# A hybrid layer on one core: the recurrence is solved in blocks, a convolution group moves to the front, and its taps and sums move to VectorE

## The chip, the cores and the metric

The kernel runs on 1 core of a Trainium2 chip. A core has four compute engines that work side by side and wait for one another through semaphores: TensorE (PE, matrix products), VectorE (DVE), ScalarE (ACT) and GpSimd (POOL). Transfers are issued from queues, here mostly that of SyncE (SP). Every engine takes its instructions in the order in which they were written into its queue, so an instruction that waits holds up all that stand behind it on that engine. The metric is the time of one execution in microseconds (us), as the device measures it; lower is better.

## The reference, cut to what matters

The input is 512 frames of 2048 channels. The first half of the layer is the part that the change touches:

```
h = rms_norm(x);  [u | v | g] = h @ W_in                # 1024 channels each
A:  bu = B u;  h[t] = lam * h[t-1] + bu[t]               # complex, 64 groups x 64 states, per frame
    y  = gelu(Re(C h) + D u);  y = y * sigmoid(y @ W_glu)
B:  z  = v * sigmoid(g);  z = causal depthwise conv of 31 taps;  layer norm over 1024 channels;  silu
x = x + rms_norm(concat(A, B) @ W_out)
```

A feed-forward part with its own up and down projections and a convolution of 3 taps follows; it is not changed.

## The kernel before, in words

Channels lie on the 128 partitions and frames along the free dimension, so a tile of 128x512 holds 128 channels of all frames. Every large product runs in three passes (`gemm`, L121 to L123): a weight block `wraw` of 128x1024 is split by ScalarE into a rounded part `wh` (L101) and by VectorE into the rest `wl` (L102), and TensorE adds `wh` times both parts of the activations and `wl` times the first. One such block, a *weight tile* below, feeds 24 products of 512 columns. There are two buffers each of `wh` and `wl` and three of `wraw`. Up to the start of the second part of the output projection VectorE splits 72 weight tiles: 48 of `w_in` (six groups of four 128-channel outputs, 8 tiles each), 8 of `w_glu`, 16 of the first half of `w_out`.

The input projection has two groups for `u` (state space) and four for `v` and `g` (value and gate). In the program the `u` groups come first (`pu0`, L222, then L467), then the four value and gate groups (L575). The norm factor `rx` (L281) is ready once the first group's input is through.

The state space works in chunks of T = 8 frames, NC = 64 of them. GpSimd computes the powers of lambda and the coefficient tables `cst`, `cy`, `cf` (helpers at L245 and L249). The products of B are spread over partitions by small transfers (`wscr`, L404) and multiplied out on VectorE (L413 to L418, 48 instructions, tiles `bx`, `by`, `btw`). `u_evac` (L447) scales a group by `rx`, sends it through memory into another layout and fills the state tile `st`, [128, 2, 32, 64] (real and imaginary, 32 pairs, 64 chunks). Then the recurrence walks over the chunks:

```python
    for c in range(NC - 1):                                    # 63 steps, L472
        ve.tensor_tensor(out=sa, in0=st[:, :, :, c], in1=lr8, op=MUL)
        ve.tensor_tensor(out=sx, in0=st[:, ::-1, :, c], in1=lam8[:, 1:3], op=MUL)
        ve.tensor_tensor(out=sa, in0=sa, in1=st[:, :, :, c + 1], op=ADD)
        scan_end = ve.tensor_tensor(out=st[:, :, :, c + 1], in0=sa, in1=sx, op=ADD).ins
```

Behind it the states go to memory (`sscr`, L516) and come back in another layout (L521); eight blocks of products (L530, L531) and a GELU give the output of the state space, which goes through memory again (`yscr`, L539) into `yall` (L541). L585 splits it into `yh` and `yl` for the `w_glu` product.

`vg_evac` (L546) evacuates a value and gate group (L551, L554 on VectorE, sigmoid on ScalarE), multiplies both on GpSimd (L557) and runs 31 taps for each of its two 128-channel blocks. The first tap is on ScalarE, the others are one VectorE instruction each (L572) that is not issued before `scan_end`. Of the eight blocks, block 3 (`PCONV`) takes another way: ScalarE scales (`pt`, L568) and GpSimd adds (L569). The layer norm sums over the blocks on GpSimd (L608, L610, L623); L617, L628 and L632 on VectorE finish it.

What sets the order: the program is written as above with priorities (weight splits, evacuations and the coefficient chain are preferred), and a scheduler fixes each engine's order before the run.

Of the kernel before, what the change touches and what calls it, by code (L numbers as in the profile page):

```python
# [32 lines left out]
PCONV = (3,)  # L33
# [26 lines left out]
def layer_kernel(ctx, tc, a, out):  # L60
# [110 lines left out]
    lam8 = const.tile([P, 3, NQ], F32, name="lam8")  # L171
# [16 lines left out]
    for i in range(2):  # L188
        for o, v in ((xts[0][:, i], a["x"][:, i]), (w0[:, S * i:S * i + S], a["w_in"][0, 0][:, S * i:S * i + S])):
# [32 lines left out]
    pu0 = gemm(wing[0], xrhs, w0, xuse)  # L222
# [322 lines left out]

    def vg_evac(ps, i0):  # L546
        zs = []
        for i in range(2):
            with tc.high_priority(offset=EPRI):
                gt = evt()  # L550
                ve.tensor_tensor(out=gt, in0=ps[2 * i + 1], in1=rx, op=MUL)  # L551
                se.activation(out=gt, in_=gt, func=AF.Sigmoid)
                vt = evt()
                ve.tensor_tensor(out=vt, in0=ps[2 * i], in1=rx, op=MUL)  # L554
            z = cv.tile([P, CK - 1 + S], F32, name="z", bufs=5)
            ge.memset(z[:, 0:CK - 1], 0.0)
# [1 line left out]
            zs.append(z)
        for k in range(CK):
            for i in range(2):  # L560
                c = i0 + i
                w = convw[:, c, k:k + 1]
                zk = zs[i][:, k:k + S]
                if k == 0:
                    se.activation(out=csb[:, c, :], in_=zk, func=AF.Copy, scale=w)
# [464 lines left out]
```

## Time and profile before

| | us |
|---|---|
| median of three runs (2088.94 to 2093.76) | 2091.67 |
| profiled execution, its own time | 2092.54 |
| span in that execution, first to last instruction | 2090.6 |
| TensorE busy | 1956.1 (94%) |
| VectorE busy | 1506.4 (72%) |
| ScalarE busy | 827.8 (40%) |
| GpSimd busy | 343.8 (16%) |
| mean granted clock of TensorE | 0.970 |

The profile is of one execution. Busy time is counted per engine, and a share over the whole span mixes parts with different limits: the changed part lies in the first 556 us, and the windows of these are what to read. The granted clock is a share of full speed: 1.00 is 2.4 GHz, and a stretch at the lower of the two levels, 1.2 GHz, counts as 0.50. The profiled time and the span differ by 1.9 us.

### The profile page before, as it was taken

How to read it: one execution, taken by the hardware profiler on the slowest of the kernel's cores; microseconds unless marked ns; L12 is line 12 of the kernel's file. 1: busy time of each engine (PE TensorE's matmuls, PEld its weight loads, DVE VectorE, ACT ScalarE, POOL GpSimd, SP SyncE). 2: the span in 40 equal slices, each digit the busy share in tenths (PEclk: the TensorE clock that was granted, in tenths of full speed). 3: DMA queues.
4: the chain of work that ended last, by engine and by line, in shares of the span. 5: the costliest groups of instructions: out<-in, count | busy, mean ns of one | idle time of the engine just before them, and what ended most of it. 6: DMA issues, size and time to landing. Idle time of an engine off the chain costs nothing. (4 is left out here: it accounts for less than half of the span.)

```text
span 2090.6 us, 30295 instructions
## 1 busy us (share of the span) xinstructions
PE 1956.1 (94%) x12070; PEld 1746.7 (84%) x12070; DVE 1506.4 (72%) x1947; ACT 827.8 (40%) x1050; POOL 343.8 (16%) x367
## 2 busy tenths in 40 slices
PE   7867988799998889999999999999999999999995
PEld 6656777678786779999999999999997888888884
DVE  5388999999536898787777878778783555555545
ACT  5111233433545544444444444444444322222223
POOL 6655143401122000000000000000000000000004
PEclk9988999999998999999999999999999999999997
DMA  6674667422226547767677676776736333333322
GB/s 211 172 222 156 213 186 209 122 86 96 91 93 175 160 152 222 204 190 210 182 199 195 194 210 184 201 197 191 207 117 225 123 131 113 119 119 123 101 94 88
DMA packets 141357, 338.80 MB, mean 162 GB/s; under 512 B 31392, under 2 KB 52896, under 8 KB 140704
## 3 DMA queue, kind: packets, MB, share of 16 engines
q1 hardware_dynamic: 123072, 289.41, 41.6%
q0 software_dynamic: 13392, 45.36, 12.5%
q10 hardware_dynamic: 4752, 2.11, 0.5%
q8 instruction: 94, 1.54, 0.3%
q14 instruction: 47, 0.39, 0.1%
HBM read 304.12 MB, written 32.70 MB: 161 GB/s over the span
## 5 line engine op out<-in xcount | busy, mean ns | idle before, releaser
L102 DVE TENSOR_TENSOR wl<-wraw,wh 128x1024 fp32r<-128x1024 f32 (+1 forms) x193 | 251.0, 1301 | 243.1 <-ACT wh L101 237.8
L101 ACT CAST wh<-wraw 128x1024 fp32r<-128x1024 f32 (+1 forms) x193 | 201.7, 1046 | 509.0 <-PE mm L122 455.1
L123 PE MATMUL mm<-hl,wl 128*128 128x512 f32 x832 | 312.0, 408 | 60.8 <-DVE wl L102 60.7
L815 PE MATMUL mm<-hl,wl 128*128 128x256 f32 x1280 | 362.9, 284 | 4.4 <-DVE wl L808 4.4
L813 PE MATMUL mm<-hl,wh 128*128 128x256 f32 x1280 | 363.1, 284 | 2.1 <-ACT wh L807 1.5
L814 PE MATMUL mm<-hl,wh 128*128 128x256 f32 x1280 | 362.9, 283 | 0.0
L121 PE MATMUL mm<-hl,wh 128*128 128x512 f32 x832 | 333.7, 406 | 24.9 <-ACT wh L101 16.1
L122 PE MATMUL mm<-hl,wh 128*128 128x512 f32 x832 | 331.8, 402 | 0.0
L121 PE MATMUL mm<-hidh,wh 128*128 128x512 f32 x704 | 275.1, 392 | 4.6 <-ACT hidh L912 4.6
L122 PE MATMUL mm<-hidl,wh 128*128 128x512 f32 x704 | 274.8, 390 | 0.0
L123 PE MATMUL mm<-hidh,wl 128*128 128x512 f32 x704 | 258.4, 390 | 0.0
L123 PEld LDWEIGHTS mm<-hl,wl 128*128 128x128 f32 x832 | 162.6, 196 | 105.6 <-DVE wl L102 70.6
L815 PEld LDWEIGHTS mm<-hl,wl 128*128 128x128 f32 x1280 | 246.4, 193 | 4.6 <-DVE wl L808 4.6
L813 PEld LDWEIGHTS mm<-hl,wh 128*128 128x128 f32 x1280 | 246.4, 193 | 2.6 <-ACT wh L807 1.7
L814 PEld LDWEIGHTS mm<-hl,wh 128*128 128x128 f32 x1280 | 246.4, 193 | 0.0
L121 PEld LDWEIGHTS mm<-hl,wh 128*128 128x128 f32 x832 | 162.4, 196 | 61.4 <-ACT wh L101 18.2
L808 DVE TENSOR_TENSOR wl<-s,wh 128x1024 fp32r<-128x1024 f32 x117 | 143.2, 1224 | 87.5 <-ACT wh L807 87.5
L807 ACT CAST wh<-wraw 128x1024 fp32r<-128x1024 f32 x120 | 125.8, 1048 | 183.5 <-PE mm L814 180.7
L807 ACT CAST wh<-s 128x1024 fp32r<-128x1024 f32 x117 | 122.8, 1049 | 175.9 <-DVE s L864 92.7
L122 PEld LDWEIGHTS mm<-hl,wh 128*128 128x128 f32 x832 | 162.2, 195 | 35.7 <-issue 0.6
L572 DVE SCALAR_TENSOR_TENSOR csb<-z,c_conv_w,csb 128x512 f32<-128x512 f32 x210 | 182.3, 927 | 0.0
L808 DVE TENSOR_TENSOR wl<-wraw,wh 128x1024 fp32r<-128x1024 f32 x120 | 146.7, 1223 | 24.8 <-ACT wh L807 21.9
(277 smaller groups left out, 3541.1 us busy)
## 6 DMA issues: line engine op xcount, KB each, us to landing
wraw<-in_ffn_w_down SPq DMA_DIRECT2D x88, 512.0 KB, 3.2
wraw<-in_ffn_w_quad SPq DMA_DIRECT2D x80, 512.0 KB, 6.2
s<-in_ffn_w_quad SPq DMA_DIRECT2D x78, 512.0 KB, 3.3
s<-in_ffn_w_quad POOLq DMA_DIRECT2D x78, 512.0 KB, 7.9
wraw<-in_w_in SPq DMA_DIRECT2D x47, 512.0 KB, 4.7
rb<-in_ffn_w_quad SPq DMA_DIRECT2D x40, 512.0 KB, 7.6
wraw<-in_w_out SPq DMA_DIRECT2D x32, 512.0 KB, 3.3
fscr<-tmp SPq DMA_DIRECT2D x44, 256.0 KB, 5.2
```

Source lines behind the costliest of these rows:

```text
L101: se.copy(out=h[:, o], in_=raw[:, o])
L102: ve.tensor_tensor(out=l[:, o], in0=raw[:, o], in1=h[:, o].bitcast(F32), op=SUB)
L121: pe.matmul(ps[m], wh[:, kk, m, :], xh, start=k == 0, stop=False)
L122: pe.matmul(ps[m], wh[:, kk, m, :], xl, start=False, stop=False)
L123: pe.matmul(ps[m], wl[:, kk, m, :], xh, start=False, stop=k == nk - 1)
L572: ve.scalar_tensor_tensor(out=csb[:, c, :], in0=zk, scalar=w, in1=csb[:, c, :], op0=MUL, op1=ADD)
L807: se.copy(out=h, in_=raw)
L808: ve.tensor_tensor(out=l, in0=raw, in1=h.bitcast(F32), op=SUB)
L813: pe.matmul(o, h[:, k, :], xh_[:, k, :], start=first and k == 0, stop=False, skip_group_check=True)
L814: pe.matmul(o, h[:, k, :], xl_[:, k, :], start=False, stop=False, skip_group_check=True)
L815: pe.matmul(o, l[:, k, :], xh_[:, k, :], start=False, stop=last and k == 7, skip_group_check=True)
```

## The change

Four things change together.

1. **Blocked recurrence.** A table `lp` holds the first eight powers of lambda to the 8th (18 more small products on GpSimd and one sign change). The recurrence runs over eight blocks of eight chunks: first inside all blocks at once (7 steps of 4 instructions, each on 512 elements per partition in place of 64), then from block to block (7 steps of 4, again 512). 252 instructions become 56.
2. **Order.** The first value and gate group is the first group of the input projection; both `u` groups follow. Its gate (`vg_gate`) comes right behind `rx`, and its taps write a tile of their own (`csb0`) and no longer have to wait for the end of the recurrence (`c > 1` alone does).
3. **Taps and gates on VectorE.** The 30 taps of block 3 that ScalarE and GpSimd shared and the eight products of value and gate move to VectorE.
4. **Norm sums on VectorE.** The seven sums over blocks and the seven over squares move there from GpSimd.

```diff
-    pu0 = gemm(wing[0], xrhs, w0, xuse)
+    pv0 = gemm(wing[2], xrhs, w0, xuse)
...
     rx = rsqrt_bcast([ssq], D)
+    def vg_gate(ps):
+        zs = []
+        for i in range(2):
+            with tc.high_priority(offset=EPRI):
+                gt = evt()
+                ve.tensor_tensor(out=gt, in0=ps[2 * i + 1], in1=rx, op=MUL)
+                se.activation(out=gt, in_=gt, func=AF.Sigmoid)
+                vt = evt()
+                ve.tensor_tensor(out=vt, in0=ps[2 * i], in1=rx, op=MUL)
+            z = zp.tile([P, CK - 1 + S], F32, name="z", bufs=4)
+            ge.memset(z[:, 0:CK - 1], 0.0)
+            ve.tensor_tensor(out=z[:, CK - 1:], in0=vt, in1=gt, op=MUL)
+            zs.append(z)
+        return zs
+    def cs_(c):
+        return csb0[:, c, :] if c < 2 else csb[:, c - 2, :]
+    def vg_taps(zs, i0):
+        for k in range(CK):
+            for i in range(2):
+                c = i0 + i
+                w = convw[:, c, k:k + 1]
+                zk = zs[i][:, k:k + S]
+                if k == 0:
+                    se.activation(out=cs_(c), in_=zk, func=AF.Copy, scale=w)
+                else:
+                    with ExitStack() as order:
+                        if c > 1:
+                            order.enter_context(tc.issue_after(scan_end))
+                        ve.scalar_tensor_tensor(out=cs_(c), in0=zk, scalar=w, in1=cs_(c), op0=MUL, op1=ADD)
+    zs0 = vg_gate(pv0)
...
+    for n in (1, 2, 4):
+        o, x = slice(n, 2 * n), slice(0, n)
+        yr, yi = (lp[:, c, :, n - 1:n].broadcast_to([P, NQ, n]) for c in (0, 2))
+        tt(pa[:, :, 0:n], lp[:, 0, :, x], yr, MUL)
...
-    u_evac(pu0, 0)
+    u_evac(gemm(wing[0], xrhs), 0)
     u_evac(gemm(wing[1], xrhs), 4)
...
-    for c in range(NC - 1):
...
+    sb = st.rearrange("p r q (s i) -> p r q s i", i=NB8)
+    for i in range(1, NB8):
+        sa = sc.tile([P, 2, NQ, NS8], F32, name="sa")
+        sx = sc.tile([P, 2, NQ, NS8], F32, name="sx")
+        ve.tensor_tensor(out=sa, in0=sb[:, :, :, :, i - 1],
+                         in1=lp[:, 0:1, :, 0:1].broadcast_to([P, 2, NQ, NS8]), op=MUL)
+        ve.tensor_tensor(out=sx, in0=sb[:, ::-1, :, :, i - 1],
+                         in1=lp[:, 1:3, :, 0:1].broadcast_to([P, 2, NQ, NS8]), op=MUL)
+        ve.tensor_tensor(out=sa, in0=sa, in1=sb[:, :, :, :, i], op=ADD)
+        ve.tensor_tensor(out=sb[:, :, :, :, i], in0=sa, in1=sx, op=ADD)
+    for b in range(1, NS8):
+        sa = sc.tile([P, 2, NQ, NB8], F32, name="sa")
+        sx = sc.tile([P, 2, NQ, NB8], F32, name="sx")
+        ve.tensor_tensor(out=sa, in0=sb[:, :, :, b - 1, NB8 - 1:NB8].broadcast_to([P, 2, NQ, NB8]),
+                         in1=lp[:, 0:1].broadcast_to([P, 2, NQ, NB8]), op=MUL)
...
+        scan_end = ve.tensor_tensor(out=sb[:, :, :, b, :], in0=sa, in1=sx, op=ADD).ins
...
-            ge.tensor_tensor(out=z[:, CK - 1:], in0=vt, in1=gt, op=MUL)
...
-                elif c in PCONV:
-                    pt = cv.tile([P, S], F32, name="pt", bufs=1)
-                    se.activation(out=pt, in_=zk, func=AF.Copy, scale=w)
-                    ge.tensor_tensor(out=csb[:, c, :], in0=csb[:, c, :], in1=pt, op=ADD)
...
-        ge.tensor_tensor(out=cs, in0=cs, in1=csb[:, i], op=ADD)
+        ve.tensor_tensor(out=cs, in0=cs, in1=cs_(i), op=ADD)
...
-            ge.tensor_tensor(out=vs, in0=vs, in1=sq, op=ADD)
+            ve.tensor_tensor(out=vs, in0=vs, in1=sq, op=ADD)
```

Line numbers move with it: L105 now splits the weights, L320 holds the taps, L295, L298 and L301 the gate, L503 the evacuation of `u`, L464 to L469 the B products, L526 to L540 the recurrence, L618 the split of `yall`. From the last additions to the output projection on, the feed-forward part included, every engine's order is that of before.

Three places of VectorE's queue show what moves. The first is right behind `rx`: in the kernel before, weight splits and the evacuation of the first `u` group stand there, and then the queue reaches the B products (L413, L414).

```order
L102 TENSOR_TENSOR wl<-wraw,wh 128x1024 x2
L452 TENSOR_TENSOR evt<-mm,rr 128x64x8 x3
L102 TENSOR_TENSOR wl<-wraw,wh 128x1024
L452 TENSOR_TENSOR evt<-mm,rr 128x64x8
L102 TENSOR_TENSOR wl<-wraw,wh 128x1024 x2
L470 MEMSET s_895 128x64
L475 TENSOR_TENSOR sa<-s_895,lam_99 128x64
L476 TENSOR_TENSOR sx<-s_895,lam_99 128x64
L102 TENSOR_TENSOR wl<-wraw,wh 128x1024
L413 TENSOR_TENSOR tmp<-k_710,s_701 128x512
```

In the changed kernel the gate of the first group and then its taps stand there, between the weight splits:

```order
L105 TENSOR_TENSOR wl<-wraw,wh 128x1024 x2
L295 TENSOR_TENSOR evt<-mm,rr 128x512
L298 TENSOR_TENSOR evt<-mm,rr 128x512
L301 TENSOR_TENSOR z<-evt 128x512
L295 TENSOR_TENSOR evt<-mm,rr 128x512
L298 TENSOR_TENSOR evt<-mm,rr 128x512
L320 SCALAR_TENSOR_TENSOR csb_103<-z,c_conv_w,csb_103 128x512
L105 TENSOR_TENSOR wl<-wraw,wh 128x1024
L301 TENSOR_TENSOR z<-evt 128x512
L320 SCALAR_TENSOR_TENSOR csb_103<-z,c_conv_w,csb_103 128x512 x5
L105 TENSOR_TENSOR wl<-wraw,wh 128x1024
L320 SCALAR_TENSOR_TENSOR csb_103<-z,c_conv_w,csb_103 128x512 x6
```

What moved: the evacuation of `u` now stands some 40 rows further on, and taps fill the rows around the weight splits. Of the 60 taps of this group, 27 stand ahead of the first B product.

The second place is the end of the recurrence. Before, its last step is followed by the taps of the first group:

```order
L475 TENSOR_TENSOR sa<-s_895,lam_99 128x64
L476 TENSOR_TENSOR sx<-s_895,lam_99 128x64
L477 TENSOR_TENSOR sa<-sa,s_895 128x64
L478 TENSOR_TENSOR s_895<-sa,sx 128x64
L572 SCALAR_TENSOR_TENSOR csb<-z,c_conv_w,csb 128x512 x2
L551 TENSOR_TENSOR evt<-mm,rr 128x512
L554 TENSOR_TENSOR evt<-mm,rr 128x512
L572 SCALAR_TENSOR_TENSOR csb<-z,c_conv_w,csb 128x512
L102 TENSOR_TENSOR wl<-wraw,wh 128x1024
L572 SCALAR_TENSOR_TENSOR csb<-z,c_conv_w,csb 128x512 x5
L102 TENSOR_TENSOR wl<-wraw,wh 128x1024
L572 SCALAR_TENSOR_TENSOR csb<-z,c_conv_w,csb 128x512 x6
```

In the changed kernel the last block step is followed by the taps of the second group:

```order
L537 TENSOR_TENSOR sx<-s_940,lp 128x512
L539 TENSOR_TENSOR sa<-sa,s_940 128x512
L105 TENSOR_TENSOR wl<-wraw,wh 128x1024
L540 TENSOR_TENSOR s_940<-sa,sx 128x64x8
L535 TENSOR_TENSOR sa<-s_940,lp 128x512
L537 TENSOR_TENSOR sx<-s_940,lp 128x512
L539 TENSOR_TENSOR sa<-sa,s_940 128x512
L540 TENSOR_TENSOR s_940<-sa,sx 128x64x8
L320 SCALAR_TENSOR_TENSOR csb<-z,c_conv_w,csb 128x512 x2
L105 TENSOR_TENSOR wl<-wraw,wh 128x1024
L320 SCALAR_TENSOR_TENSOR csb<-z,c_conv_w,csb 128x512 x6
L105 TENSOR_TENSOR wl<-wraw,wh 128x1024
```

What moved: 33 weight tiles are split ahead of the end of the recurrence before, 37 in the changed kernel, so the recurrence ends four weight tiles later in the row.

The third place is the split of the state-space output (before L585, now L618; tile `hl`). Before, the first six of the eight splits stand behind 13 weight tiles, counted from the end of the recurrence, and the last two behind 15; these are the first six:

```order
L102 TENSOR_TENSOR wl<-wraw,wh 128x1024
L572 SCALAR_TENSOR_TENSOR csb<-z,c_conv_w,csb 128x512
L585 TENSOR_TENSOR hl<-s_1827,hl 128x512
L572 SCALAR_TENSOR_TENSOR csb<-z,c_conv_w,csb 128x512
L585 TENSOR_TENSOR hl<-s_1827,hl 128x512 x2
L572 SCALAR_TENSOR_TENSOR csb<-z,c_conv_w,csb 128x512
L585 TENSOR_TENSOR hl<-s_1827,hl 128x512 x3
L572 SCALAR_TENSOR_TENSOR csb<-z,c_conv_w,csb 128x512 x3
```

In the changed kernel the first four stand behind ten weight tiles:

```order
L105 TENSOR_TENSOR wl<-wraw,wh 128x1024
L320 SCALAR_TENSOR_TENSOR csb<-z,c_conv_w,csb 128x512 x5
L105 TENSOR_TENSOR wl<-wraw,wh 128x1024
L320 SCALAR_TENSOR_TENSOR csb<-z,c_conv_w,csb 128x512 x3
L618 TENSOR_TENSOR hl<-s_1822,hl 128x512 x2
L320 SCALAR_TENSOR_TENSOR csb<-z,c_conv_w,csb 128x512
L618 TENSOR_TENSOR hl<-s_1822,hl 128x512 x2
L320 SCALAR_TENSOR_TENSOR csb<-z,c_conv_w,csb 128x512 x2
L105 TENSOR_TENSOR wl<-wraw,wh 128x1024
L320 SCALAR_TENSOR_TENSOR csb<-z,c_conv_w,csb 128x512
L643 TENSOR_TENSOR ssq<-ssq,csb 128x512
L320 SCALAR_TENSOR_TENSOR csb<-z,c_conv_w,csb 128x512 x2
```

What moved: counted from the end of the recurrence, the first four splits stand three weight tiles earlier; the fifth and sixth stand behind 12 and 13 tiles, and the last two behind 15 as before. Taps and the first norm sums (L643) fill the rows between.

## Rows read from the trace of the kernel before

**Rows 1.** Windows of the first 556 us: busy time per engine (instructions), granted clock.

```profile
core 0: us, PE busy (x) PEld busy (x) DVE busy (x) ACT busy (x) POOL busy (x), PEclk, DMA share, GB/s
58.00:64.00 6.00, 6.00 (x27) 4.69 (x25) 5.03 (x1) 1.98 (x2) 5.92 (x8) 1.00 0.51 169
64.00:121.00 57.00, 41.32 (x220) 33.17 (x220) 22.43 (x29) 8.08 (x10) 24.00 (x29) 0.85 0.87 216
121.00:192.00 71.00, 49.36 (x355) 38.58 (x353) 65.03 (x63) 10.84 (x13) 57.42 (x40) 0.89 0.56 175
192.00:267.00 75.00, 69.91 (x404) 55.45 (x405) 71.43 (x250) 18.97 (x22) 7.72 (x9) 0.97 0.60 195
267.00:400.00 133.00, 112.56 (x584) 94.63 (x583) 133.00 (x138) 52.52 (x67) 58.12 (x38) 0.92 0.61 177
400.00:515.00 115.00, 108.63 (x467) 86.83 (x468) 113.07 (x141) 39.86 (x51) 16.89 (x8) 1.00 0.33 106
515.00:556.00 41.00, 37.86 (x166) 30.71 (x165) 24.38 (x30) 22.00 (x32) 11.34 (x7) 0.96 0.20 72
```

**Rows 2.** What TensorE waited for, 64 to 295 us: total, times, longest.

```profile
PE mm L123 <- DVE wl L102: 32.5, 7, 11.3
```

**Rows 3.** The same list, 295 to 556 us.

```profile
PE mm L123 <- DVE wl L102: 19.4, 10, 8.2
PE mm L121 <- ACT wh L101: 3.9, 1, 3.9
PE mm L121 <- DVE evt L551: 3.1, 1, 3.1
```

**Rows 4.** VectorE groups by line, 0 to 560 us: busy us, mean ns.

```profile
L572 DVE SCALAR_TENSOR_TENSOR csb<-z,c_conv_w,csb 128x512 f32<-128x512 f32 x210 | 182.3, 927 | 0.0
...
L475 DVE TENSOR_TENSOR sa<-s,lam 128x64 f32<-128x64 f32 x63 | 22.8, 362 | 2.1
...
L585 DVE TENSOR_TENSOR hl<-s,hl 128x512 fp32r<-128x512 f32 x8 | 8.3, 1071 | 0.0
L604 DVE TENSOR_TENSOR hl<-tmp,hl 128x512 fp32r<-128x512 f32 x8 | 5.5, 687 | 0.0
```

**Rows 5.** VectorE timeline, 58 to 296 us: start, us, instruction, [idle before].

```profile
58.97 5.47 DVE L102 TENSOR_TENSOR wl<-wraw,wh 128x1024 fp32r<-128x1024 f32 x1 [4.74 <-ACT wh L101]
...
156.81 1.06 DVE L452 TENSOR_TENSOR evt<-mm,rr 128x512 f32<-128x512 f32 x1
...
174.44 1.49 DVE L477 TENSOR_TENSOR sa<-sa,s 128x64 f32<-128x64 f32 x1
...
295.13 1.22 DVE L102 TENSOR_TENSOR wl<-wraw,wh 128x1024 fp32r<-128x1024 f32 x1
```

**Rows 6.** VectorE timeline, a stretch of taps while GpSimd is idle.

```profile
497.96 1.23 DVE L102 TENSOR_TENSOR wl<-wraw,wh 128x1024 fp32r<-128x1024 f32 x1
499.09 4.07 DVE L572 SCALAR_TENSOR_TENSOR csb<-z,c_conv_w,csb 128x512 f32<-128x512 f32 x6
```

**Rows 7.** VectorE timeline, 554 to 592 us: weight splits of the output projection.

```profile
554.78 1.22 DVE L102 TENSOR_TENSOR wl<-wraw,wh 128x1024 fp32r<-128x1024 f32 x1 [0.91 <-ACT wh L101]
...
584.98 1.22 DVE L102 TENSOR_TENSOR wl<-wraw,wh 128x1024 fp32r<-128x1024 f32 x1 [3.23 <-ACT wh L101]
...
590.42 1.23 DVE L102 TENSOR_TENSOR wl<-wraw,wh 128x1024 fp32r<-128x1024 f32 x1 [4.22 <-ACT wh L101]
```

**Rows 8.** TensorE timeline: products of the state-space output.

```profile
284.15 0.39 PE L531 MATMUL aux<-tmp,cst 128*128 128x64 f32 x2
284.37 0.39 PE L530 MATMUL aux<-um,k 128*128 128x64 f32 x2
```

**Rows 9.** GpSimd groups by line, 0 to 680 us: power products.

```profile
L245 POOL TENSOR_TENSOR pab<-lamr,lami 128x32 f32<-128x32 f32 (+2 forms) x3 | 1.1, 367 | 0.1
```

**Rows 10.** SyncE queue timeline: way of the state-space output through memory.

```profile
266.80 5.47 SPq L516 DMA_DIRECT2D sscr<-s  x4
...
404.56 0.81 SPq L541 DMA_DIRECT2D s<-yscr  x2
```

More of the change, by code (lines that the diff above doesn't have):

```diff
@@ L32 @@
 NEVT = 3
-PCONV = (3,)
 WPRI = 4000
@@ L40 @@
 HS = S // 2
+NB8 = 8
+NS8 = NC // NB8
 NX = 3
@@ L64, in layer_kernel @@
     const = ctx.enter_context(tc.tile_pool(name="const", bufs=1))
+    lead = ctx.enter_context(tc.tile_pool(name="lead", bufs=1))
+    lead.tile([P, 96], F32, name="lead")
     constr = ctx.enter_context(tc.tile_pool(name="constr", side="right", bufs=1))
@@ L162, in layer_kernel @@
     p2 = ph1.enter_context(tc.tile_pool(name="p2", bufs=1, reuse_waits="tile"))
+    zp = ph1.enter_context(tc.tile_pool(name="zp", bufs=1, reuse_waits="tile"))
+    csb0 = zp.tile([P, 2, S], F32, name="csb0")
+    sc = ph1.enter_context(tc.tile_pool(name="sc", bufs=1, reuse_waits="tile"))
+    lp = sc.tile([P, 3, NQ, NB8], F32, name="lp")
     prep = ExitStack()
@@ L169, in pload @@
         return t
-    lam8 = const.tile([P, 3, NQ], F32, name="lam8")
     xh = [hl16.tile([P, 8, S], F32R, name="hl") for _ in range(2)]
@@ L188, in layer_kernel @@
     for i in range(2):
-        for o, v in ((xts[0][:, i], a["x"][:, i]), (w0[:, S * i:S * i + S], a["w_in"][0, 0][:, S * i:S * i + S])):
+        for o, v in ((xts[0][:, i], a["x"][:, i]), (w0[:, S * i:S * i + S], a["w_in"][2, 0][:, S * i:S * i + S])):
             with ExitStack() as order:
@@ L306, in layer_kernel @@
         ts(lami[:, :, t], sn[:, o], -1.0, 1.0, MUL, MUL)
-    tt(lam8[:, 0], mag[:, NQ:], sh[:, NQ:], MUL)
-    ge.tensor_copy(out=lam8[:, 2], in_=sn[:, NQ:])
-    ts(lam8[:, 1], sn[:, NQ:], -1.0, 1.0, MUL, MUL)
+    tt(lp[:, 0, :, 0], mag[:, NQ:], sh[:, NQ:], MUL)
+    ge.tensor_copy(out=lp[:, 2, :, 0], in_=sn[:, NQ:])
     pab = pp.tile([P, 8 * NQ], F32, name="pab")
@@ L379, in layer_kernel @@
     pri.close()
+    for n in (1, 2, 4):
+        o, x = slice(n, 2 * n), slice(0, n)
+        yr, yi = (lp[:, c, :, n - 1:n].broadcast_to([P, NQ, n]) for c in (0, 2))
+        tt(pa[:, :, 0:n], lp[:, 0, :, x], yr, MUL)
+        tt(pb[:, :, 0:n], lp[:, 2, :, x], yi, MUL)
+        tt(lp[:, 0, :, o], pa[:, :, 0:n], pb[:, :, 0:n], SUB)
+        tt(pa[:, :, 0:n], lp[:, 0, :, x], yi, MUL)
+        tt(pb[:, :, 0:n], lp[:, 2, :, x], yr, MUL)
+        tt(lp[:, 2, :, o], pa[:, :, 0:n], pb[:, :, 0:n], ADD)
+    ge.tensor_scalar(out=lp[:, 1], in0=lp[:, 2], scalar1=-1.0, scalar2=1.0, op0=MUL, op1=MUL)
     prep.close()
@@ L544, in layer_kernel @@
     csb = cv.tile([P, 8, S], F32, name="csb")
[L546 to L556, printed above, removed]
-            ge.tensor_tensor(out=z[:, CK - 1:], in0=vt, in1=gt, op=MUL)
[L558 to L565, printed above, removed]
-                elif c in PCONV:
-                    pt = cv.tile([P, S], F32, name="pt", bufs=1)
-                    se.activation(out=pt, in_=zk, func=AF.Copy, scale=w)
-                    ge.tensor_tensor(out=csb[:, c, :], in0=csb[:, c, :], in1=pt, op=ADD)
-                else:
-                    with tc.issue_after(scan_end):
-                        ve.scalar_tensor_tensor(out=csb[:, c, :], in0=zk, scalar=w, in1=csb[:, c, :],
-                                                op0=MUL, op1=ADD)
-    for i in range(4):
-        vg_evac(gemm(wing[2 + i], xrhs), 2 * i)
+    vg_taps(zs0, 0)
+    for i in range(1, 4):
+        vg_taps(vg_gate(gemm(wing[2 + i], xrhs)), 2 * i)
     yh = hl16.tile([P, 8, S], F32R, name="hl")
```

22 lines of the change are left out of this document (9 added, 13 removed).

## The prediction

> **What bounds the kernel now.** I read the windows first. From 121 to 515 us VectorE is busy nearly all the time: 65.0 of 71, 71.4 of 75, 133.0 of 133 and 113.1 of 115 us, while TensorE has gaps and part of its stretches run at the lower clock (granted 0.85 to 0.92 in three windows, that is partly 1.2 in place of 2.4 GHz) [rows 1]. The list of waits says which gaps: between 64 and 295 us TensorE waits 32.5 us for the weight split `wl`, between 295 and 556 us another 19.4 us, and 7.0 us for `wh` and a gate evacuation [rows 2, 3]. The reader is to see that the split itself is short (1.13 us from its start to the next instruction in the queue [rows 6]) and comes late because VectorE's other work stands ahead of it. So up to the layer norm the kernel goes at VectorE's pace. Only 22.4 of the 57 us from 64 to 121 are used there [rows 1]: the work that could fill them, the taps, is bound to the end of the recurrence.
>
> From the first tile of the output projection's second half (the 73rd weight tile, split at 554.78 us [rows 7]) TensorE sets the pace: splits come 5.44 us apart and wait for TensorE to free a buffer [rows 7]. The order behind that point stays. The question is therefore how much earlier tile 73 comes.
>
> **The change, costed.** What it removes from VectorE: 252 small instructions of the recurrence (four lines of 63; with the tiles and gates between them they fill the window 192 to 267 and a little before [rows 1, 4]). What it adds there: 56 instructions of 512 elements, 30 taps, 8 products for the gate and 14 sums. In GpSimd's place nothing is left of these from 267 us on, where it was busy 58.1 + 16.9 us up to 515 [rows 1].
>
> That matters because VectorE is slow while GpSimd works. A tap alone takes 0.66 us ((4.07 - 0.08) / 6, or 0.745 with its overlap [rows 6]), but the mean over 210 is 0.927 us [rows 4]: 210 x 0.18 = 38 us lost, with some 3 us on splits 41 us for 75 us of GpSimd work, 0.55 us for each. All of this goes away. But the 60 taps that move ahead now run beside GpSimd's coefficient work: 24.0 + 57.4 us busy after 64 us [rows 1] and 19 new power products at 0.367 us [rows 9], 7 us, together 88 us. At 0.55 that is 49 us. Bounds: 0, if VectorE works in GpSimd's pauses, and 88 us, if it always waits.
>
> *First half, to the split of weight tile 37* (the last before the end of the new recurrence; before, it is split at 295.1 us [rows 5]). I add up VectorE's row of the changed kernel from the first gate on, which can start at 64.4 us, when the split that starts at 58.97 ends [rows 5]:
>
> - 28 weight splits x 1.13 = 31.6 [rows 6]
> - 60 taps x 0.66 = 39.6 [rows 6]
> - 48 B products and 13 gate instructions and sums x 0.60 = 36.6 (a plain product of 512 takes 0.687 with its overlap [rows 4])
> - 8 evacuations of `u` x 1.0 = 8.0 [rows 5]
> - first loop of the recurrence, 28 x 0.99 = 27.7: its tiles are read and written with a step of 8 elements. No row has that step; the nearest is the strided split at 1.071 against 0.687 us for a contiguous one [rows 4]. I take the strided price; the bound below is 0.60, 11 us less in all
> - second loop up to this tile, 23 x 0.63 = 14.5 (runs of 8 elements; 0.60 and a little for the dependence; bound above 0.99, 8 us more)
>
> Together 158 us. To this the 49 us, and waits: 3 us for the sigmoid that now stands in VectorE's own row, 4 us for a B load, and 10 us at the start of the recurrence. There the states of the last `u` block come back through memory: before, 17.6 us lie between the last evacuation and the first addition that needs them [rows 5], and the changed row has only 5.6 us of work between these two. Tile 37 then comes at 64.4 + 158 + 49 + 17 = 288.6 us, 6.5 us earlier than before. The taps in the idle stretch are paid for by GpSimd's work beside them, so this half gains little.
>
> *Second half, tile 37 to tile 73.* Before it takes 554.8 - 295.1 = 259.7 us [rows 5, 7]. TensorE needs 36 x 5.44 = 195.8 us for the tiles, 28.6 us for 256 products of the state-space output (two in 0.22 us [rows 8]) and some 2 us for the norm: 226 us. The other 33 us are its waits (26.4 [rows 3]) and the lower clock (8% of 133 us [rows 1]). In the changed row VectorE has 184 us of work between the recurrence and the layer norm, against 192 us of TensorE's for the 30 tiles in that piece: still 96% full. A row that full let TensorE lose 6.4 of 115 us before (400 to 515, busy 108.6 [rows 1]), which gives 13 us over 226. The moved sums cost 14 x 0.60 = 8.4 us in VectorE's row, counted in the 184 or hidden under TensorE's last tiles before tile 73.
>
> The state-space output is late next. Before, its last read-back is issued 404.56 - 266.80 = 138 us after the first store of the states [rows 10]; its last splits stand behind 15 weight tiles in both rows. With 15 tiles at 5.44 us, the 28.6 us and their part of the 13 us, TensorE is there after some 115 us. SyncE's queue holds this traffic and the weight loads in one row, so that it mostly goes at the pace of the tiles; the wait is between 0 and 138 + 3 - 115 = 26 us. Queued behind it on VectorE are weight splits for `w_glu`. I take 8 us, nearer to 0, because SyncE waits for free weight buffers between these steps. So 226 + 13 + 8 = 247 us, 13 us less than before.
>
> Sum: 6.5 + 13 = 19 us. The profiled execution took 2092.5 us (its span and 1.9 us around it); the median of the runs shown is 0.9 us lower. 2092.5 - 19 - 0.9 = 2072.6, so **2073 us**.
>
> **A rule against the change.** The rows give 0.55 us of VectorE for each us of GpSimd [rows 1, 4]. The Trainium skill (SBUF — State Buffer, "SBUF: two separate sides") says that VectorE and GpSimd share a pair of ports as an exclusive lock held for a whole instruction, and that the loser "fully blocks". By that rule, taken at its hardest, the 88 us of coefficient work cost 88 us and not 49, and the sum is a loss of 20 us, 2112 us. The mean of the taps here disagrees with the hardest reading.
>
> **Rivals.**
>
> 1. *Little lock, no new wait.* GpSimd pauses for its own loads, and the taps fall into the pauses: 20 in place of 49 us, and the state-space output comes in time (8 us less). Gain 19 + 29 + 8 = 56 us: 2036 us. For it: GpSimd is busy only 24.0 of 57 us in the first window. Against: it worked almost without a pause (5.92 of 6 us [rows 1]) just before the point where the taps now begin.
> 2. *The state-space output becomes the wait.* SyncE's way through memory keeps its 138 us: 18 us more than I take, gain 1 us, 2092 us, the same as before. For it: eight small stores and two loads per pair stay as they are. Against: much of the 138 us went by while SyncE waited for weight buffers.
> 3. *The lock decides, slower.* Place: VectorE's row from 64 us to the first B products and on to the recurrence, beside `cst` and `cy`. If a us of GpSimd costs 0.9 us, the price is 79 us and the sum a loss of 11 us: 2103 us. It decides from 0.77 us on, tile 37 later than 308 us. For it: the split that began at 58.97 us took 5.47 in place of 1.2 us while GpSimd was busy 5.92 of 6 us [rows 1, 5, 6]. Against: the mean of 210 taps.
> 4. *It doesn't do what it says:* something outside the changed part holds the time. No row speaks for it, since the projections behind run at TensorE's pace.
>
> **How the numbers follow.** Forecast 0.44 (2058 to 2087), rival 1 0.24, rival 2 0.13, rival 3 0.15, rival 4 0.04. What a measurement of this kernel can tell from no change is about 0.2%, 4 us. Rival 2 falls about evenly on faster, same and slower, rival 3 on slower but for 0.02, rival 4 on the same: faster 0.71, same 0.11, slower 0.18. The range goes from 2040, near rival 1, to 2100, near rival 3.
>
> **What would show it.** Tile 37 at about 289 us and tile 73 at about 536 us in VectorE's timeline; taps at 0.66 us behind the recurrence and above 1 us ahead of it; first-loop instructions at about 1.07 us; TensorE's waits for `wl` below 10 us behind the recurrence, and a stop of VectorE at L618 of 0 to 26 us. Wrong I am if tile 37 comes outside 265 to 310 us, if VectorE stands for more than 15 us at L618, or if taps beside GpSimd cost as little as alone.

## The result, and the profile after

The changed kernel takes 2068.05 us (median of four runs, 2067.19 to 2071.05), the kernel before 2092.4 us on the same chip (median of four runs, the three of the table ahead and a fourth): a ratio of 0.9893, with an interval of 0.9881 to 0.9905. The forecast was 2073 us. The profiled execution took 2071.05 us with a span of 2069.3 us, 21.3 us less than that of before.

VectorE's timeline at the two places of the sum (start, duration, instruction; in brackets the idle time before it and what ended it) answers to [rows 5, 7]:

```profile
294.78 1.22 DVE L105 TENSOR_TENSOR wl<-wraw,wh 128x1024 fp32r<-128x1024 f32 x1
...
533.44 1.23 DVE L105 TENSOR_TENSOR wl<-wraw,wh 128x1024 fp32r<-128x1024 f32 x1
```

Weight tile 37 is split at 294.78 us, before at 295.13: the first half gains 0.4 us, where 6.5 was forecast. Tile 73 is split at 533.44, before at 554.78: 21.3 us are won in all, and the second half gains 21 where 13 was forecast. From there on the distance between the two kernels stays near 20 us.

The windows of the changed kernel, which answer to [rows 1]:

```profile
core 0: us, PE busy (x) PEld busy (x) DVE busy (x) ACT busy (x) POOL busy (x), PEclk, DMA share, GB/s
64.00:121.00 57.00, 40.88 (x162) 32.25 (x163) 53.50 (x56) 10.34 (x12) 44.20 (x43) 0.88 0.60 150
121.00:192.00 71.00, 53.64 (x312) 41.52 (x310) 68.35 (x61) 10.74 (x12) 49.95 (x33) 0.90 0.64 192
192.00:267.00 75.00, 62.84 (x437) 49.81 (x438) 60.33 (x57) 13.47 (x16) 16.49 (x15) 0.89 0.59 176
267.00:400.00 133.00, 128.74 (x668) 109.87 (x667) 122.72 (x171) 37.44 (x42) 1.46 (x3) 0.93 0.73 214
400.00:515.00 115.00, 114.72 (x519) 94.48 (x518) 106.86 (x143) 50.06 (x68) 0.00 (x0) 1.00 0.33 108
515.00:556.00 41.00, 41.00 (x190) 34.19 (x189) 21.47 (x31) 23.27 (x33) 0.00 (x0) 1.00 0.29 92
```

Two things have changed. From 64 to 121 us VectorE is now nearly full (53.5 of 57 us in place of 22.4), and GpSimd's busy time there has grown from 24.0 to 44.2 us, although of work only the power products were added, some 7 us. From 267 us on GpSimd is empty and TensorE works 128.74 of 133 and 114.72 of 115 us: there it has become the bound. The waits say the same. From 64 to 295 us TensorE waits for the split as long as before [rows 2]:

```profile
PE mm L126 <- DVE wl L105: 31.6, 12, 5.7
PE aux L411 <- POOL cf L251: 8.5, 2, 7.1
```

and from 295 to 556 us almost nothing is left of [rows 3], 0.2 us for the split in place of 19.4:

```profile
PE aux L593 <- DMA tmp<-sscr: 2.9, 1, 2.9
PE aux L592 <- DMA k<-kscr: 1.4, 1, 1.4
PE mm L126 <- DVE wl L105: 0.2, 1, 0.2
```

What VectorE pays for one instruction is in its groups (busy us, mean ns, idle time before). The first fence is the stretch from 60 to 206 us, ahead of the recurrence, the second 206 to 285 us with the recurrence, the third 285 to 440 us behind it:

```profile
L320 DVE SCALAR_TENSOR_TENSOR csb<-z,c_conv_w,csb 128x512 f32<-128x512 f32 x51 | 61.8, 1258 | 0.0
L105 DVE TENSOR_TENSOR wl<-wraw,wh 128x1024 fp32r<-128x1024 f32 x15 | 28.9, 1929 | 4.9 <-ACT wh L104 4.9
...
L464 DVE TENSOR_TENSOR tmp<-k,s 128x512 f32<-128x512 f32 x4 | 2.8, 688 | 6.0 <-issue 3.4 <-DMA k<-in_ssm_bT 2.7
```

```profile
L526 DVE TENSOR_TENSOR sa<-s,lp 128x512 f32<-128x512 f32 x7 | 8.0, 1136 | 3.3 <-ACT s L514 3.0
...
L535 DVE TENSOR_TENSOR sa<-s,lp 128x512 f32<-128x512 f32 x3 | 2.1, 691 | 0.1
```

```profile
L320 DVE SCALAR_TENSOR_TENSOR csb<-z,c_conv_w,csb 128x512 f32<-128x512 f32 x131 | 90.2, 748 | 0.0
L105 DVE TENSOR_TENSOR wl<-wraw,wh 128x1024 fp32r<-128x1024 f32 x21 | 25.7, 1224 | 9.0 <-ACT wh L104 9.0
L618 DVE TENSOR_TENSOR hl<-s,hl 128x512 fp32r<-128x512 f32 x8 | 8.4, 1072 | 1.3 <-ACT hl L617 1.3
```

The same tap costs 1258 ns beside GpSimd's work and 748 ns without it (0.08 of that is overlap with the next one). The first loop of the recurrence, whose tiles have a step of 8 elements, costs 1.11 to 1.14 us an instruction, the second 0.69. At L618, where a wait of up to 26 us was feared, VectorE stands for 1.3 us.

### The profile page after: what moved, and what is told of

Its sections match the earlier page's. It is cut to its first block, busy times and chain, and to the rows that moved or that the text cites. A ratio compares the mean times of both kernels' runs of the same rounds, so it can differ in the third digit from the quotient of the medians.

```text
span 2069.3 us, 30081 instructions
## 1 busy us (share of the span) xinstructions
PE 1956.1 (95%) x12070; PEld 1751.0 (85%) x12070; DVE 1501.2 (73%) x1803; ACT 810.3 (39%) x1022; POOL 280.9 (14%) x333
## 5 line engine op out<-in xcount | busy, mean ns | idle before, releaser
L105 DVE TENSOR_TENSOR wl<-wraw,wh 128x1024 fp32r<-128x1024 f32 (+1 forms) x193 | 248.8, 1289 | 239.6 <-ACT wh L104 238.9
L320 DVE SCALAR_TENSOR_TENSOR csb<-z,c_conv_w,csb 128x512 f32<-128x512 f32 x240 | 192.3, 857 | 0.1
```

The lines of the kernel that those rows point to most:

```text
L105: ve.tensor_tensor(out=l[:, o], in0=raw[:, o], in1=h[:, o].bitcast(F32), op=SUB)
L320: ve.scalar_tensor_tensor(out=cs_(c), in0=zk, scalar=w, in1=cs_(c), op0=MUL, op1=ADD)
```

## The experiments

All twelve in one table. The ratio is to the kernel before, run on the same chip beside it. The last three columns are starts of weight splits in VectorE's timeline (us): tile 37, tile 73, and tile 80, which is behind the layer norm. The kernel before took 2090.9 to 2092.6 us beside the twelve, so differences between two of these kernels are good to some 2 us. The columns are each of one execution; tile 37 stands near the end of the new recurrence in the changed kernel, but not at the same place in every row (runs 1 and 7).

| Kernel | us | ratio, interval | 37 | 73 | 80 |
|---|---|---|---|---|---|
| before | 2092.4 | 1 | 295.1 | 554.8 | 590.4 |
| changed | 2068.1 | 0.9893, 0.9881 to 0.9905 | 294.8 | 533.4 | 569.9 |
| 1 old recurrence | 2079.9 | 0.9945, 0.9928 to 0.9961 | 287.0 | 542.0 | 578.8 |
| 2 taps behind | 2095.7 | 1.0017, 1.0003 to 1.0030 | 283.9 | 526.8 | 589.7 |
| 3 GpSimd again | 2102.1 | 1.0053, 1.0038 to 1.0068 | 306.3 | 563.1 | 601.1 |
| 4 third of tables | 2043.1 | 0.9771, 0.9757 to 0.9786 | 269.8 | 505.0 | 541.2 |
| 5 reorder alone | 2115.7 | 1.0112, 1.0097 to 1.0127 | 298.3 | 578.3 | 616.4 |
| 6 VectorE alone | 2074.8 | 0.9924, 0.9905 to 0.9944 | 281.6 | 517.4 | 570.3 |
| 7 tables on VectorE | 2046.1 | 0.9779, 0.9765 to 0.9794 | 264.4 | 509.3 | 545.2 |
| 8 half the taps behind | 2078.4 | 0.9941, 0.9919 to 0.9963 | 286.5 | 523.2 | 577.2 |
| 9 sums on GpSimd | 2070.5 | 0.9891, 0.9874 to 0.9907 | 293.1 | 533.3 | 569.4 |
| 10 = 7, powers too | 2038.1 | 0.9748, 0.9732 to 0.9764 | 253.9 | 497.1 | 539.9 |
| 11 = 6, tables too | 2058.7 | 0.9849, 0.9834 to 0.9863 | 257.2 | 504.3 | 558.2 |
| 12 = 7, half the taps behind | 2057.0 | 0.9837, 0.9819 to 0.9855 | 265.4 | 501.5 | 554.4 |

My theory A was the account of the prediction: VectorE's row is what counts up to tile 37, a us of GpSimd's busy time costs it about 0.45 there, and behind the recurrence TensorE sets the pace. The rivals are named in the text of each run: that one part alone is the whole gain (the blocks, the early taps, or GpSimd's absence behind the recurrence), that the early taps are slow for another reason than GpSimd, or that the recurrence isn't on the path. After the first four runs (1 to 4) I took A2 in place of A: the parts act on one thing, VectorE's row, and there are two deadlines for it, the splits up to tile 73 and the layer norm behind it. After the next four I added L: operations of GpSimd and VectorE exclude each other.

**1. The recurrence of 63 steps again.**

```diff
-    for i in range(1, NB8):
...
-    for b in range(1, NS8):
...
+    for c in range(NC - 1):
+        ve.tensor_tensor(out=sa, in0=st[:, :, :, c], in1=lr8, op=MUL)
...
```

> The changed kernel with the recurrence of before (63 steps of four small instructions) and without the 19 power products. Theory A (VectorE's row sets the first half, each us there counts): the 63 steps cost VectorE about 61 us by the rows of before, the two loops take 49 us in the changed kernel, so the row is 12 us longer; the power products leave GpSimd, 7 us at about 0.45 are 3 us back. Tile 37 (or the tile that then comes last before the end of the recurrence) and tile 73 some 9 us later: 2072 to 2082 us. Rival B (the blocked recurrence is the whole gain): 2088 us or more. Rival D (TensorE, not the recurrence, sets the pace there): within 3 us of 2068.

It took 2079.87 us, 12 more than the changed kernel, and tile 73 comes 8.5 us later: theory A by its numbers, and both rivals are out. (Tile 37 comes 7.8 us earlier because it stands further ahead in the longer recurrence, which ends at 317.8 us in place of 299.3.) Blocking the recurrence is worth what it saves VectorE.

**2. and 8. All, or half, of the early taps bound to the end of the recurrence.** The diff is that of run 8; in run 2 the condition is gone.

```diff
-                        if c > 1:
+                        if c > 1 or k > 15:
                             order.enter_context(tc.issue_after(scan_end))
```

> The changed kernel with the first two blocks' taps bound to the end of the recurrence, as all taps were before; all else, the first gate and value group in front too, stays. Theory A: 51 taps at 1.19 us beside GpSimd (61 us) leave VectorE's row ahead of 206 us and come back as 51 at 0.667 us (34 us) behind the recurrence, so the work is 27 us less in all, but behind the recurrence VectorE's row goes from 213 to 247 us of work and becomes the bound there. Recurrence ends 20 to 45 us earlier, tile 73 within 10 us of the changed kernel: 2058 to 2078 us. Rival B (putting taps into the idle stretch is what brings the gain): tile 73 some 20 to 34 us later, 2088 to 2102 us.

> The changed kernel with the upper half of the first two blocks' taps (32 of 60) bound to the end of the recurrence. With all 60 bound, tile 73 came 7 us earlier and the layer norm 26 us later. Theory A2 (two deadlines: the weight splits and, behind tile 73, the end of VectorE's row before the norm; the row has some 20 us of slack there): tile 73 2 to 8 us earlier, TensorE waits at the norm below 8 us, 2060 to 2074 us. Rival B (each early tap is a gain): half of the 28 us lost with all of them bound, 2079 to 2085 us.

Run 2 took 2095.68 us (median of ten, 2087.79 to 2097.91; the profiled one took 2089.45): theory A's time is wrong and its rival's is right. But the rival's place is wrong: tile 73 comes 6.7 us earlier, as A has it, and the time is lost behind it. TensorE's waits in run 2, 515 to 570 us:

```profile
PE aux L139 <- DVE tmp L654: 11.6, 1, 11.6
PE mm L124 <- ACT hl L662: 4.0, 1, 4.0
PE aux L152 <- DVE rs L149: 1.4, 1, 1.4
```

L139 sums the squares for the layer norm, and waits for VectorE's last addition. In the changed kernel TensorE waits for nothing in this stretch. VectorE's row behind the recurrence is then so full of taps that the norm is late, while the splits, which have a higher priority, are in time. Run 8 says the same with half the taps: tile 73 is 10.2 us earlier, TensorE waits 6.8 us at L139 and 12.2 us in all there, and the time is 2078.39. A2 forecast 2074 at most and its rival 2079 at least; neither has it, A2 since the wait at the norm is longer than it said. From tile 73 to tile 80 the changed kernel takes 36 us, run 2 takes 63, run 8 takes 54.

The waits are not the whole of it. The windows from tile 73 to tile 80, first of the changed kernel, then of run 2, with the part of run 2 around the end of its longest wait (543.75 us) ahead of it:

```profile
533.44:569.87 36.43, 36.43 (x162) 30.20 (x161) 15.35 (x18) 19.89 (x29) 3.96 (x3) 1.00 0.31 101
```

```profile
541.00:556.00 15.00, 6.73 (x22) 5.40 (x23) 9.45 (x20) 9.12 (x15) 0.00 (x0) 0.50 0.00 0
526.75:589.69 62.94, 45.82 (x188) 36.92 (x187) 32.53 (x49) 33.16 (x48) 3.96 (x3) 0.81 0.17 59
```

Of the 27 us that run 2 takes more, 17 are waits and 9 are longer work: towards the end of the 11.6 us in which TensorE stands its granted clock falls, and from 541 to 556 us it is 0.50, the lower of the two levels. So a late norm costs the wait and some clock behind it; in run 8 it is 12 and 5 us.

**3. and 9. All of part three undone; the norm sums alone.** PCONV is block 3 again, and the sums of squares go back too (left out of the diff as shown); run 9 has the sums alone.

```diff
-            ve.tensor_tensor(out=z[:, CK - 1:], in0=vt, in1=gt, op=MUL)
+            ge.tensor_tensor(out=z[:, CK - 1:], in0=vt, in1=gt, op=MUL)
...
+                elif c in PCONV:
...
+                    se.activation(out=pt, in_=zk, func=AF.Copy, scale=w)
+                    ge.tensor_tensor(out=cs_(c), in0=cs_(c), in1=pt, op=ADD)
...
-        ve.tensor_tensor(out=cs, in0=cs, in1=cs_(i), op=ADD)
+        ge.tensor_tensor(out=cs, in0=cs, in1=cs_(i), op=ADD)
...
```

> The changed kernel with block 3's taps on ScalarE and GpSimd, the gate products and the norm sums on GpSimd, as before. Theory A: VectorE sheds 52 instructions, some 33 us, and pays about 0.45 to 0.55 of GpSimd's 75 us there, 34 to 41 us, so its row changes by 0 to 8 us; it stands idle 26 of 239 us there and TensorE sets the pace, so the time stays within 5 us of 2068. Rival E (freeing VectorE of GpSimd behind the recurrence is the gain of the second half): tile 73 15 to 25 us later, 2083 us or more; taps behind the recurrence at 0.8 us and above.

> The changed kernel with the 14 norm sums alone back on GpSimd; taps and gate products stay on VectorE. By the prediction's own term (the moved sums cost 8.4 us that lie hidden under TensorE's last tiles before tile 73): within 4 us of 2068. Rival (the norm is the second deadline: 13 sums in two chains take some 1.6 us each on GpSimd beside VectorE and 0.6 on VectorE, so the norm comes later and TensorE waits for it): 2074 to 2084 us, and then part of the 34 us of undoing all of part three is from the sums.

Run 3 took 2102.06 us, 34 more: theory A falls here and its rival holds. VectorE sheds 52 instructions, and is no less busy for it. GpSimd's and VectorE's main groups in run 3, 306 to 400 us, where the taps are:

```profile
L320 POOL TENSOR_TENSOR csb<-csb,pt 128x512 f32<-128x512 f32 x19 | 35.3, 1860 | 36.2 <-ACT pt L319 36.2
```

```profile
L325 DVE SCALAR_TENSOR_TENSOR csb<-z,c_conv_w,csb 128x512 f32<-128x512 f32 x76 | 71.7, 986 | 0.7
```

and the windows:

```profile
267.00:400.00 133.00, 117.18 (x590) 97.68 (x588) 129.78 (x134) 52.24 (x66) 58.07 (x35) 0.92 0.59 174
400.00:515.00 115.00, 106.06 (x463) 88.02 (x462) 103.20 (x125) 44.40 (x58) 20.29 (x14) 0.91 0.36 116
```

Taps take 986 ns in place of 748, and one of GpSimd's additions 1860 ns. The mistake in A was to set the sum of relief and price against the idle time of the whole stretch: 58 of GpSimd's 78 us fall between 267 and 400 us, where VectorE is then 129.8 of 133 us busy and TensorE loses 16 us of 133. Of the 30 us at tile 73, 11 are there by the end of the recurrence, which starts as early as in the changed kernel (237.6 against 238.0 us): GpSimd's additions for block 3 begin beside it. Run 9 (2070.5 us) shows that the sums have no part in it: they lie hidden, as the prediction has it.

**4. and 7. The price of GpSimd's table products.** Run 4 leaves out 32 of the 48 table products and sums; run 7 computes all 48 on VectorE. The diff is that of run 7 (`tt` is GpSimd); run 4 leaves out the second and third line.

```diff
-            tt(ct[:, ri], cq(cin[:, 0]), lq(l0), MUL)
-            tt(cy, cq(cin[:, 1]), lq(l1), MUL)
-            tt(ct[:, ri], ct[:, ri], cy, op)
+            ve.tensor_tensor(out=ct[:, ri], in0=cq(cin[:, 0]), in1=lq(l0), op=MUL)
+            ve.tensor_tensor(out=cy, in0=cq(cin[:, 1]), in1=lq(l1), op=MUL)
+            ve.tensor_tensor(out=ct[:, ri], in0=ct[:, ri], in1=cy, op=op)
```

> The changed kernel with the table of the state-space output formed from one product in place of two products and a sum: 32 of 48 GpSimd instructions are left out (the output is then another). Theory A (early taps are slow because GpSimd works beside them): some 54 us of GpSimd's work leave the stretch up to 206 us; at 0.45 that is 24 us of VectorE's row. Taps ahead of the recurrence fall from 1.26 us to 1.0 or less, tile 37 comes 12 to 24 us earlier, time 2044 to 2058 us. Rival C (the early taps are slow for another reason, their operands or the transfers beside them): they stay above 1.2 us, tile 37 moves by less than 5 us, 2064 to 2070 us.

> The changed kernel with the 48 products and sums of 576 elements for the state-space table on VectorE, not GpSimd; the output is the same. Theory A2: VectorE's row gets 48 x 0.68 = 33 us of work and loses the slowing by some 81 us of GpSimd at 0.45, 36 us; tile 37 within 8 us of the changed kernel's, 2060 to 2076 us. A price of 0.8 or more a us would give tile 37 30 us earlier and 2040 us or less. The Trainium skill (SBUF, its section on the two sides of SBUF) has the loser fully blocked; by that the gain is near 48 us.

Run 4 took 2043.08 us with tile 37 25 us earlier, a little more than A's bounds, and the rival is out: what slows the early taps is GpSimd. Run 7 took 2046.05 us, 22 less, where A2 gave 8 at most: its price of 81 x 0.45 / 48 = 0.76 us for a table product is too low. The 48 us of the expectation's last sentence did not come either; it charged 81 us of GpSimd's busy time, waits included. Tile 73 is 24 us earlier. (Tile 37 is 30 us earlier, but it stands 18 us ahead of the recurrence's end there and 4 in the changed kernel, so tile 73 is the place to compare.) VectorE's groups of run 7, 60 to 206 us:

```profile
L320 DVE SCALAR_TENSOR_TENSOR csb<-z,c_conv_w,csb 128x512 f32<-128x512 f32 x50 | 36.7, 763 | 0.0
L105 DVE TENSOR_TENSOR wl<-wraw,wh 128x1024 fp32r<-128x1024 f32 x21 | 26.9, 1283 | 0.5 <-ACT wh L104 0.5
L487 DVE TENSOR_TENSOR cst<-cst,cy 128x576 f32<-128x576 f32 x13 | 10.2, 784 | 0.0
```

Why the price is higher is seen where the two engines work side by side. GpSimd's, then VectorE's timeline of the changed kernel, 196 to 202 us:

```profile
196.66 1.61 POOL L251 TENSOR_TENSOR cst<-cin,lami 128x576 f32<-128x576 f32 x1
198.24 1.61 POOL L251 TENSOR_TENSOR cy<-cin,lami 128x576 f32<-128x576 f32 x1
```

```profile
195.60 1.65 DVE L320 SCALAR_TENSOR_TENSOR csb<-z,c_conv_w,csb 128x512 f32<-128x512 f32 x1
197.17 1.65 DVE L469 TENSOR_TENSOR csb<-csb,tmp 128x512 f32<-128x512 f32 x1
198.75 1.65 DVE L468 TENSOR_TENSOR csb<-csb,tmp 128x512 f32<-128x512 f32 x1
```

and GpSimd's in run 3, at a time when VectorE has nothing to do:

```profile
69.89 1.16 POOL L252 TENSOR_TENSOR cy<-cin,lami 128x576 f32<-128x576 f32 x1
71.01 1.16 POOL L252 TENSOR_TENSOR cst<-cin,lami 128x576 f32<-128x576 f32 x1
```

Alone, a table product takes 1.16 us and a tap or sum 0.60 to 0.66. Side by side each takes some 1.6 us, and in 1.58 us one of each is done: they take turns, and nothing overlaps but some 0.2 us at the ends. So a table product costs VectorE 1.58 - 0.60 = 0.98 us while they take turns, and GpSimd's row shows 1.61 us busy, 0.45 of which is its own waiting.

VectorE's whole row gives the mean over all of them. From 128.19 to 206.20 us it works without a pause on 7 splits, 18 taps, 34 B products and sums and 4 evacuations of `u` (0.93 us each when alone). At their prices alone that is 44 us; the other 34 fall to 36 table products and sums that GpSimd does there and one product of 256 elements, 0.92 us each. The check is the stretch from 110.77 to 125.46 us, where GpSimd has nothing to do: 14 products and sums, 6 taps and 2 splits, 14.6 us by the same prices, 14.7 in the trace.

On VectorE the same product costs 0.70 us (0.784 with its overlap of 0.08). For 48 that is, as an estimate, 44 us against 34, a gain of 10. Another 6 us are VectorE's own waits: from 64 to 267 us it is idle for 20.8 us in the changed kernel and for 14.4 in run 7 (203 us less 44.09 + 71.00 + 73.50 busy). That is 16 of the 24 us at tile 73; the rest is not taken apart.

**5. and 6. Parts of the change by themselves.** Run 5 is the changed kernel with the edits of runs 1 and 3 together, so that only the order is left. Run 6 is the kernel before with part three alone:

```diff
-PCONV = (3,)
+PCONV = ()
...
-            ge.tensor_tensor(out=z[:, CK - 1:], in0=vt, in1=gt, op=MUL)
+            ve.tensor_tensor(out=z[:, CK - 1:], in0=vt, in1=gt, op=MUL)
...
```

> Of the change only the new order is left (first gate and value group in front, its taps free to run early); the recurrence of 63 steps and GpSimd's share of taps, gates and norm sums are those of before. Undone one at a time these two cost 12 and 34 us. Theory A2 (all three parts lengthen or shorten the same thing, VectorE's row up to the layer norm, so their prices add): 2107 to 2121 us, slower than before. Rival B (early taps in the idle stretch are a gain of their own, whatever the rest does): 2065 to 2086 us.

> The kernel before with only the third part of the change: block 3's taps, gate products and norm sums on VectorE. Theory A2 (a full row on VectorE takes 33 us of new work and loses 36 to 41 us of slowing by GpSimd, measured by the first of these runs; what decides is the row up to the layer norm): 2076 to 2092 us. Rival E (GpSimd beside the taps costs more than its price on VectorE, as its undoing at 34 us says): 2056 to 2072 us.

Run 5 took 2115.67 us, 23 more than before: the order alone is a loss, and undone one by one the prices add, as A2 has it. Run 6 took 2074.8 us (2071.97 to 2079.47), 1 us below A2's bound and 3 above that of its rival, so it decides for neither: part three alone brings 18 of the 24 us. At tile 73 it is even ahead of the changed kernel (517.4 against 533.4), and gives this back at the norm, where TensorE waits 7.0 us for VectorE and then 4.0 for the first normed tile:

```profile
PE aux L136 <- DVE tmp L623: 7.0, 1, 7.0
PE mm L121 <- ACT hl L631: 4.0, 1, 4.0
PE aux L149 <- DVE rs L146: 1.4, 1, 1.4
```

So that is what order and blocks are for: they let 60 taps go ahead, and the norm comes in time.

**10, 11 and 12. Whether this leads to a better kernel.** Run 10 moves the other products of powers, coefficients and B from GpSimd to VectorE as well, run 11 puts the tables on VectorE in run 6 (without the new order and the blocks), run 12 binds half of the early taps in run 7. The edits are those shown (in run 10 `ve.tensor_tensor` for `tt` in 48 more instructions).

> The tables on VectorE as in the run of 2046 us, and with them the remaining products of powers, coefficients and B (48 products and sums of 32 to 512 elements, forty-eight GpSimd instructions). Theory L (GpSimd's and VectorE's operations exclude each other, one us of GpSimd alone costs a full VectorE one us): these hold GpSimd for some 20 us alone and VectorE for about 13; and the table products waited 10.4 us for the powers from GpSimd, which come sooner now. 2030 to 2044 us. Rival (a chain of small dependent instructions in VectorE's own queue holds the weight splits up): 2046 us or more.

> The kernel before with only taps, gates, norm sums and the 48 table products on VectorE: no new order, no blocked recurrence. Theory L: with part three alone the time was 2074.8 and tile 73 at 517, but the layer norm came late, as all 240 taps stand behind the recurrence. The table products on VectorE (34 us, in a stretch where it is busy 20 of 57 us) free it of some 50 us of GpSimd's, the recurrence starts up to 20 us earlier: 2052 to 2068 us, so 6 us or more slower than the same step on the changed kernel, which is then what order and blocks are worth. Rival (order and blocks are worth nothing once GpSimd is out of the way): 2050 us or less.

> The tables on VectorE as in the run of 2046 us, and the upper half of the first two blocks' taps bound to the end of the recurrence. In the changed kernel itself this cost 10 us: tile 73 came 10 us earlier and the norm 17 us later against it. Now early taps cost 0.66 us, the same as late ones, so nothing is saved ahead by moving them but some 20 us more stand behind: 2050 to 2062 us. Rival (what counts is the weight splits ahead of 267 us, where VectorE is full): 2036 to 2044 us.

All three fall where theory L puts them, on which they were forecast: the two engines exclude each other, and there are two deadlines, the splits and the norm. Run 10 is the fastest kernel, 2038.14 us, 53 us under before and 30 under the change. In it GpSimd is busy for 6.39 us from 64 to 121 us and TensorE for 46.8 in place of 40.9. With the tables off GpSimd, order and blocks are worth 13 us (run 11 against run 7), and the upper half of the early taps 11 us (run 12).

## Why the prediction was right, point by point

**The sign and the size were right**, 19 us forecast and 24 measured, and the places as well: VectorE's pace up to tile 73, TensorE's behind it. The halves were off by 6 and 8 us, in opposite directions, so that the sum came out within 5 us is in part luck.

**First half: 0.4 us in place of 6.5.** From 64.4 to tile 37 the forecast was 224.2 us, measured are 230.4. By terms:
- *The first loop was 3 us too short.* From 238.00 to 272.04 us stand its 28 instructions with three splits of 1.13 us: (34.04 - 3.4) / 28 = 1.095 us, 30.6 in place of 27.7. The choice of the strided price over 0.60 was right.
- *The waits were 3.4 us too short.* VectorE stands 6.0 us for a B load, 2.7 for an evacuation, and at the start of the recurrence 2.15 + 6.46 + 3.04 us, together 20.3 in place of 17. This is the largest of them, VectorE's timeline from 226 us:

```profile
226.05 1.22 DVE L105 TENSOR_TENSOR wl<-wraw,wh 128x1024 fp32r<-128x1024 f32 x1 [2.15 <-ACT wh L104]
233.73 1.23 DVE L105 TENSOR_TENSOR wl<-wraw,wh 128x1024 fp32r<-128x1024 f32 x1 [6.46 <-ACT wh L104]
238.00 1.17 DVE L526 TENSOR_TENSOR sa<-s,lp 128x512 f32<-128x512 f32 x1 [3.04 <-ACT s L514]
```

- *The lock came out at its 49 us* (230.4 - 160.9 of work - 20.3), but by two sizes that cancel, which is luck: GpSimd shows 44.2 + 50.0 + 16.5 = 111 us busy in these windows in place of 88, and VectorE pays 0.45 for each in place of 0.55. Busy time of GpSimd was the wrong unit, since it grows with VectorE's load.
- *Slips of the working.* The row has 27 splits up to tile 37 and not 28 (1.1 us; the lock is then 50). The lower clock (8% of 133 us is 10.6) and 26.4 us of waits are 37 us and not the 33 that they were to explain in the kernel before. Rival 2's gain of 1 us is 2091 us, not 2092. Only the first enters the forecast.

**Second half: 238.7 us in place of 247.** TensorE's 226 us stand. The 13 us for a full queue and the lower clock are 4.5 us of waits (2.9 + 1.4 + 0.2) and up to 9 us of clock (0.93 over 133 us, that is in part 1.2 in place of 2.4 GHz). The 8 us for the state-space output were too many: 1.3. Rival 2, which rested on this wait, is out.

**"The order behind that point stays", and TensorE alone sets the pace from tile 73:** true of these two kernels, but runs 2, 6, 8, 11 and 12 show what it hangs on. In the changed kernel VectorE's row is through with the norm just in time; whatever stands behind the recurrence in addition is paid there. I priced the early taps by what they cost ahead, and gave them no gain but VectorE's lighter row; their worth is the norm, 28 us by the medians of run 2, 18 in the execution that its trace shows.

**"The taps in the idle stretch are paid for by GpSimd's work beside them":** shown by run 4 and run 7. This is also the rule of the Trainium skill (SBUF — State Buffer, "SBUF: two separate sides") that I set against the rows: the pair of ports is locked for a whole instruction and the other engine blocks. I let the mean of 210 taps speak against its hardest reading. The rows of run 3 and of the changed kernel side by side agree with the rule: 1.16 and 0.60 us one after the other are 1.76, and a pair takes 1.58. What was wrong was my reading, which charged GpSimd's busy time, waits included, as time of the lock. By the 0.92 us from VectorE's row the 48 table products and sums are some 44 of the 49 us (an estimate).

**Rivals.** Rival 1 (little lock) is what runs 4 and 7 make of the kernel, not what it is. Rival 3 (the lock decides) was near: tile 37 at 294.8 us with 308 as the point from which it would have been slower. Rival 4 is out by runs 1, 2 and 3: each part undone costs time.

## What to carry to other kernels

Before work is moved to GpSimd to relieve a full VectorE, compare what the product takes on VectorE alone with what it takes on GpSimd alone: here, where both read two operands, they take turns, and VectorE pays nearly all of GpSimd's time, 0.92 us in the mean for a product that takes 0.70 on VectorE itself. Read the price from a row where the other engine stands idle, not from GpSimd's busy share, which contains its own waits. And when work is put earlier or later on a full engine, look for every deadline behind it: the one that moves (the splits) may gain while the next (the norm) loses more.

## What the runs showed of the hardware that was not expected

Taking turns is not assured. In run 7, where VectorE works without a pause (71.00 of 71 us), one GpSimd product of 256 elements, where one of this size takes 0.63 us alone in run 3, was under way for 15.93 us:

```profile
162.32 15.93 POOL L553 TENSOR_TENSOR s<-s,dm 128x256 f32<-128x256 f32 x1 [4.83 <-DMA s<-in_ssm_d]
```

and the other way round, in the changed kernel as before, a split of 1.2 us stands for 5.3 us while GpSimd runs products back to back:

```profile
58.71 5.30 DVE L105 TENSOR_TENSOR wl<-wraw,wh 128x1024 fp32r<-128x1024 f32 x1 [4.91 <-ACT wh L104]
```

In both cases the engine that held the other off went from one instruction to the next without a pause. But that does not suffice: in run 3 the split at the same place, beside the same products, takes 1.37 us:

```profile
58.66 1.37 DVE L106 TENSOR_TENSOR wl<-wraw,wh 128x1024 fp32r<-128x1024 f32 x1 [4.49 <-ACT wh L105]
```

What decides between this and the even turns at 196 us is open, as no run separates it.
